# The squares of the norms: all additions but the last of each sum moved from VectorE to GpSimd

## The chip, the core and the metric

The kernel runs on one core of a Trainium2 chip. The time is that of one launch in device microseconds; the number compared is the median of several runs. The core's engines work side by side, each from a queue of its own in a fixed order: TensorE (PE; its weight loads are shown as PEld), VectorE (DVE), ScalarE (ACT), GpSimd (POOL) and SyncE (SP). They wait for each other by semaphores.

## What is computed

The program is three transformer blocks one after the other, over 512 tokens of width 1024 in fp32: a first block with three mixers and a gated feed-forward part, a second with two layers of mixers (sparse attention, convolution, latent attention, delta rule) and feed-forward parts, and a third with two recurrent mixers and a feed-forward part. What matters here is that norms over the 1024 channels stand ahead of and behind nearly every matrix product. Cut to that:

```python
def rmsnorm(x, g):
    xf = x.astype(jnp.float32)
    y = xf * lax.rsqrt(jnp.mean(xf * xf, axis=-1, keepdims=True) + NORM_EPS)
    return (y * g.astype(jnp.float32)).astype(x.dtype)

def layernorm(x, g, b):
    xf = x.astype(jnp.float32)
    mu = jnp.mean(xf, axis=-1, keepdims=True)
    var = jnp.mean(jnp.square(xf - mu), axis=-1, keepdims=True)
    y = (xf - mu) * lax.rsqrt(var + EPS) * g.astype(jnp.float32) + b.astype(jnp.float32)
    return y.astype(x.dtype)

# first block
x = x + rmsnorm(mix, post_mix_g[l])
h = rmsnorm(x, pre_ffn_g[l])
gate, up = jnp.split(h @ w_ffn_in[l], 2, axis=-1)
f = (jax.nn.silu(gate) * up) @ w_ffn_out[l]
x = x + rmsnorm(f, post_ffn_g[l])
# third block
x = _layernorm(ALPHA * x + mixed @ w_out[layer], ln1_g[layer], ln1_b[layer])
```

## The kernel before

Activations are kept transposed: a vector of 512 tokens by 1024 channels is eight tiles of 128 channels by 512 tokens. Around the norms the work is cut into two halves of 256 tokens (`HF`), so that most tiles there are 128x256. Every matrix product is split in three to keep fp32's precision: weights and activations are split into a high part and the rest (`whi`, `wlo`, `ahi`, `alo`), and TensorE multiplies low by high, high by low and high by high (lines 458 to 460, 610 to 612 and 652 to 654). A weight of 128x1024 comes by DMA into `wst`, ScalarE makes `whi` from it (line 525) and VectorE `wlo` (line 534, the helper through which VectorE's two-operand instructions go).

A norm needs the sum over channels, that is over the eight tiles and the 128 partitions of each. The class `Sums` (lines 289 to 394) does it for one half. For each tile `put` makes the square (`sq`, on ScalarE; every second one on VectorE in the first mixer) and holds it back until the next tile's turn, when `up` adds it into an accumulator `nm_as` (128x256). For a layernorm `put` also subtracts a rough mean (`nm_mb`) and a second accumulator `nm_ax` sums the values themselves. `flush` adds the last square held back; then `columns` multiplies the accumulator with a column of ones on TensorE (line 367), and some fifteen small VectorE instructions (`nm_c`, `nm2y`, `nm2t`, `nm2h`) make the reciprocal root. `rows` transposes it back into rows (line 710) for scaling (`nm_r` of an output norm, `fd_rb` of an input norm). The very last norm of the program, in its second half, feeds its last square to TensorE without the last addition (`direct`).

There are 24 such sums, six of them of layernorms (two in the convolution, two each for the two layernorms of block 3). They stand in `boundary` (lines 727 to 830), which ends one stage and begins the next: the output product's halves, their sums, the scaling and adding to `x` (through `po_t` in the first block), the split of the new `x` into `ahi` and `alo` for the next product with its own sum (`Feed`, lines 396 to 438), and the next product's first matmuls (`First`, lines 441 to 465). `boundary` writes these pieces in an order that follows estimated due times; after that the framework schedules instructions by priority and by its own estimate of each one's duration, so a changed instruction can move others in every engine's queue. The first sum of all, at the program's start, is that of the input (`x_in`).

GpSimd does little: some memsets, the DMA issues of six of the convolution's eight tiles (`ud` and `c_x`, lines 1665 and 1668), and six multiplications and additions in the last norm (lines 1798 and 1799). Its first arithmetic instruction is that of the last norm.

Of the kernel before, what the change touches and what calls it, by code (L numbers as in the profile page):

```python
# [15 lines left out]
ALU = mybir.AluOpType  # L16
# [61 lines left out]
def _consts():  # L78
    c = {}
    i = np.arange(P)  # L80
    f = np.float32
    c["ident"] = np.eye(P, dtype=f)
    caus = np.zeros((P, S), f)
    caus[:, S - P:] = np.where(i[None, :] > i[:, None], NEG, 0.0)
    c["caus"] = caus
    j = np.arange(64)
    h = i % 64
    c["eye2"] = (h[:, None] == j[None, :]).astype(f)
    up = [(h[:, None] < j[None, :]), (h[:, None] <= j[None, :])]
    c["upm"] = np.concatenate(up, 1).astype(f)  # L90
    for m in (1, 2, 4, 8, 16, 32):
        t, s = h[:, None], j[None, :]
        same = (t // (2 * m)) == (s // (2 * m))
        c[f"lev{m}"] = (same & ((t // m) % 2 == 1) & ((s // m) % 2 == 0)).astype(f)
    t, s = j[None, :], h[:, None]
    c["lev1T"] = (((t // 2) == (s // 2)) & (t % 2 == 1) & (s % 2 == 0)).astype(f)
    c["eye32"] = (i[:, None] % 32 == np.arange(32)[None, :]).astype(f)
    c["headones"] = ((i[:, None] // 64) == (i[None, :] // 64)).astype(f)
    c["headind"] = ((i[:, None] // 64) == np.arange(2)[None, :]).astype(f)
    c["triu"] = (i[:, None] <= i[None, :]).astype(f)  # L100
    c["reset"] = np.repeat((np.arange(S) % 64 > 0).astype(f)[None], P, 0)
    return c
# [186 lines left out]
class Sums:  # L289
# [22 lines left out]
    def put(self, x):  # L312
        k, i = self.k, self.count
        if self.ln:
            k.tt(x, x, self.mb, ALU.subtract)
        late, self.late = self.late, []
        if not i:
            self.acc["s"] = k.square(self.tile("s"), i, x)
            self.first = x
        else:  # L320
            pool, tags, bufs, _ = self.sqs
            sq = pool.tile([P, self.n], F32, name="sq", tag=tags[i % len(tags)], bufs=bufs)
            self.late.append(("s", k.square(sq, i, x)))
            if self.ln:
                self.late.append(("x", x))
        self.up(late)
        self.count += 1

    def up(self, late):
        k = self.k  # L330
        for what, x in late:
            if what not in self.acc:
                self.acc[what] = self.tile(what)
                k.tt(self.acc[what], self.first, x, ALU.add)
            else:
                k.tt(self.acc[what], self.acc[what], x, ALU.add)

    def flush(self, last=False):

        k, n = self.k, self.n  # L340
        if self.early:
            ps = k.bank(self.psp, "st")
            k.T.matmul(ps[:, :n], k.onesq, self.early[0], start=True, stop=True)
            self.mb = self.sp.tile([P, n], F32, name="nm_mb", bufs=2)
            k.copy(self.mb, ps[:, :n], 1.0 / P)
            for x in self.early:
                self.put(x)
            self.early = []
            yield FL, False
        if last and not self.direct:  # L350
            late, self.late = self.late, []
            self.up(late)

    def rstd(self, eps, out):

# [1945 lines left out]
```

## Time and profile before

| | us |
|---|---|
| median of three runs | 3287.34 |
| lowest and highest | 3286.98, 3298.29 |
| the profiled execution's time | 3295.74 |
| its span in the profile | 3293.7 |
| granted TensorE clock, mean | 0.992 of full speed |
| HBM read and written | 297.45 MB, 7.46 MB |

The page's first lines give each engine's busy time and share of the span. Its chain follows back from the last instruction what each one waited for. A view of waits names who waited for what in how many places; a group view adds up instructions of one line and shape, with busy time and the mean duration of one; a timeline gives start, duration, engine, line and operands, and in brackets the idle time ahead and what ended it. In windows the columns are the busy time of PE, PEld, DVE, ACT and POOL, then the granted TensorE clock.

### The profile page before, as it was taken

The page shows a single profiled execution, that of the slowest core. Times are in us where ns is not written, and L with a number is a line of the kernel's source. Part 1 is how long each engine was busy: PE and PEld are TensorE (multiplying, and loading weights), DVE is VectorE, ACT ScalarE, POOL GpSimd, SP SyncE. Part 2 cuts the span into 40 slices and gives each one's busy share as a digit, 9 for nine tenths or more (in the row PEclk, how much of TensorE's full clock was granted, in tenths as well). Part 3 has the DMA queues.
Part 4 walks back from the last instruction along what each step waited for, and adds up shares of the span by engine and source line. Part 5 has one row for each costly group of instructions (what it writes and reads, how often), then busy time and mean ns, then how long its engine had stood idle before and what let it go on. Part 6 is the DMA issues. An engine that isn't in the chain of part 4 may idle for free.

```text
span 3293.7 us, 47967 instructions
## 1 busy us (share of the span) xinstructions
PE 3238.2 (98%) x19850; PEld 2698.0 (82%) x19850; DVE 1929.5 (59%) x4109; ACT 1177.1 (36%) x1879; POOL 29.3 (1%) x99
## 2 busy tenths in 40 slices
PE   8999999999999999999999999999999999999998
PEld 6877888897879888977888897778787777998888
DVE  7567743458856444597544466574466566563336
ACT  4243533234354222335322243343343433353223
POOL 0000000000000000020000000000000000000000
PEclk9999999999999999999999999999999999999999
DMA  3210522232212222262322231112221222222322
GB/s 137 78 43 5 171 99 102 91 107 79 88 64 77 102 91 102 106 184 93 112 90 102 104 139 62 65 65 90 84 87 62 102 77 103 103 100 90 106 90 90
DMA packets 57354, 308.00 MB, mean 94 GB/s; under 512 B 7088, under 2 KB 16432, under 8 KB 24496
## 3 DMA queue, kind: packets, MB, share of 16 engines
q1 hardware_dynamic: 54736, 296.79, 25.7%
q0 software_dynamic: 2400, 8.16, 1.0%
q8 instruction: 155, 2.54, 0.3%
q14 instruction: 63, 0.52, 0.0%
HBM read 297.45 MB, written 7.46 MB: 93 GB/s over the span
## 4 chain that ended last, share of the span: by engine, by line
PE 94%; DVE 4%; ACT 1%; issue 0%; DMA 0%; POOL 0%; SPq 0%; ACTq 0%; DVEq 0%
PE mm L652 15%; PE mm L653 15%; PE mm L654 15%; PE mm L610 8%; PE mm L612 8%; PE mm L611 8%; PE mm L635 2%; PE mm L637 2%; PE mm L636 2%; PE iv L1203 2%; PE mm L458 1%; PE mm L459 1%; PE mm L460 1%; PE cv L1691 1%; PE sc L2185 1%; PE sc L1975 1%
## 5 line engine op out<-in xcount | busy, mean ns | idle before, releaser
L534 DVE TENSOR_TENSOR wlo<-wst,whi 128x1024 fp32r<-128x1024 f32 (+2 forms) x535 | 646.9, 1212 | 669.5 <-ACT whi L525 668.1
L525 ACT ACTIVATE whi<-wst 128x1024 fp32r<-128x1024 f32 (+2 forms) x535 | 559.6, 1049 | 1217.7 <-PE mm L654 632.0
L652 PE MATMUL mm<-ahi,wlo 128*128 128x512 f32 (+1 forms) x1984 | 726.4, 367 | 2.7 <-DVE x L544 1.9
L653 PE MATMUL mm<-alo,whi 128*128 128x512 f32 (+1 forms) x1984 | 726.8, 367 | 0.2 <-DVE alo L534 0.2
L654 PE MATMUL mm<-ahi,whi 128*128 128x512 f32 (+1 forms) x1984 | 725.2, 366 | 0.0
L652 PEld LDWEIGHTS mm<-ahi,wlo 128*128 128x128 f32 x1984 | 375.1, 189 | 64.3 <-DVE x L544 2.1
L653 PEld LDWEIGHTS mm<-alo,whi 128*128 128x128 f32 x1984 | 375.6, 189 | 62.9 <-issue 2.5
L654 PEld LDWEIGHTS mm<-ahi,whi 128*128 128x128 f32 x1984 | 375.4, 189 | 61.2 <-issue 1.7
L610 PE MATMUL mm<-ahi,wlo 128*128 128x512 f32 (+2 forms) x1048 | 423.3, 404 | 0.5 <-DVE d_qi L534 0.5
L612 PE MATMUL mm<-ahi,whi 128*128 128x512 f32 (+2 forms) x1048 | 408.4, 390 | 0.0
L611 PE MATMUL mm<-alo,whi 128*128 128x512 f32 (+2 forms) x1048 | 406.7, 388 | 0.0
L610 PEld LDWEIGHTS mm<-ahi,wlo 128*128 128x128 f32 (+1 forms) x1048 | 197.1, 188 | 50.0 <-issue 9.3
L612 PEld LDWEIGHTS mm<-ahi,whi 128*128 128x128 f32 (+1 forms) x1048 | 196.9, 188 | 42.1 <-issue 0.2
L611 PEld LDWEIGHTS mm<-alo,whi 128*128 128x128 f32 (+1 forms) x1048 | 197.2, 188 | 39.6 <-issue 2.5
L652 PE MATMUL mm<-hhi,wlo 128*128 128x256 f32 (+1 forms) x720 | 228.4, 317 | 0.0
L653 PE MATMUL mm<-hlo,whi 128*128 128x256 f32 (+1 forms) x720 | 228.1, 317 | 0.0
L654 PE MATMUL mm<-hhi,whi 128*128 128x256 f32 (+1 forms) x720 | 227.1, 316 | 0.0
L458 PE MATMUL mm<-ahi,wlo 128*128 128x256 f32 x512 | 144.0, 290 | 16.7 <-DVE wlo L534 10.3
L459 PE MATMUL mm<-alo,whi 128*128 128x256 f32 x512 | 146.4, 288 | 1.6 <-DVE alo L544 1.5
L460 PE MATMUL mm<-ahi,whi 128*128 128x256 f32 x512 | 145.2, 286 | 0.0
L653 PEld LDWEIGHTS mm<-hlo,whi 128*128 128x128 f32 x720 | 137.4, 191 | 8.9
L652 PEld LDWEIGHTS mm<-hhi,wlo 128*128 128x128 f32 x720 | 137.2, 191 | 9.2
(471 smaller groups left out, 4418.3 us busy)
## 6 DMA issues: line engine op xcount, KB each, us to landing
wst<-in_w2f SPq DMA_DIRECT2D x36, 1024.0 KB, 4.8
wst<-in_w2i SPq DMA_DIRECT2D x32, 1024.0 KB, 4.8
wst<-in_w1i SPq DMA_DIRECT2D x22, 1024.0 KB, 4.9
wst<-in_w3f SPq DMA_DIRECT2D x22, 1024.0 KB, 4.9
wst<-in_w1f SPq DMA_DIRECT2D x10, 1024.0 KB, 4.8
wst<-in_w3d SPq DMA_DIRECT2D x10, 1024.0 KB, 4.9
wst<-in_w1o SPq DMA_DIRECT2D x8, 1024.0 KB, 4.9
wst<-in_w2qk SPq DMA_DIRECT2D x8, 1024.0 KB, 4.9
```

Source lines behind the costliest of these rows:

```text
L458: K_.T.matmul(ps, lo[:, c], ah, start=k == 0, stop=False)
L459: K_.T.matmul(ps, hi[:, c], al, start=False, stop=False)
L460: K_.T.matmul(ps, hi[:, c], ah, start=False, stop=k == KD - 1)
L525: return self.A.activation(out, in_, func, **kw)
L534: return self.V.tensor_tensor(out, a, b, op=op)
L610: self.T.matmul(ps, lo[:, c], ah, start=k == 0, stop=False)
L611: self.T.matmul(ps, hi[:, c], al, start=False, stop=False)
L612: self.T.matmul(ps, hi[:, c], ah, start=False, stop=k == n - 1)
L635: self.T.matmul(ps, ah[:, c], lo, start=k == 0, stop=False)
L652: self.T.matmul(ps, lo[:, c], ah, start=k == 0, stop=False)
L653: self.T.matmul(ps, hi[:, c], al, start=False, stop=False)
L654: self.T.matmul(ps, hi[:, c], ah, start=False, stop=k == n - 1)
```

## The change

`up` gets the engine that adds as an argument. `put` passes GpSimd (`k.G`), `flush` passes VectorE (`k.V`) for the last addition of each sum. The instruction is written out instead of going through the helper at line 534; what that helper adds, a raised priority, was not in force at these places.

```diff
@@ put
-        self.up(late)
+        self.up(late, k.G)
         self.count += 1
 
-    def up(self, late):
-        k = self.k
+    def up(self, late, e):
         for what, x in late:
             if what not in self.acc:
                 self.acc[what] = self.tile(what)
-                k.tt(self.acc[what], self.first, x, ALU.add)
+                e.tensor_tensor(self.acc[what], self.first, x, op=ALU.add)
             else:
-                k.tt(self.acc[what], self.acc[what], x, ALU.add)
+                e.tensor_tensor(self.acc[what], self.acc[what], x, op=ALU.add)
@@ flush
         if last and not self.direct:
             late, self.late = self.late, []
-            self.up(late)
+            self.up(late, k.V)
```

In instructions: of 208 additions on VectorE 180 go to GpSimd (144 into `nm_as`, 36 into `nm_ax`), 28 stay. VectorE's queue falls from 4063 to 3883 instructions, GpSimd's grows from 104 to 284. GpSimd's set-up instruction for arithmetic moves from ahead of the last norm to the start of its queue. Lines behind 329 are one lower after the change.

The first place is the first boundary, where the output product of the first block's mixers meets the feed-forward part. VectorE before (`nm_as_4374` sums the second half of the output, `nm_as_4371` the first half of the new `x`):

```order
L544 SCALAR_TENSOR_TENSOR po_t_4532<-y6_4241,vec1_80,nm_r0_4359 128x256
L534 TENSOR_TENSOR nm_as_4371<-nm_as_4371,sq_4517 128x256
L534 TENSOR_TENSOR x6_4212<-x6_4212,po_t_4532 128x256
L544 SCALAR_TENSOR_TENSOR po_t_4554<-y7_4242,vec1_80,nm_r0_4359 128x256
L534 TENSOR_TENSOR nm_as_4374<-nm_as_4374,sq_4483 128x256
L544 SCALAR_TENSOR_TENSOR alo_4536<-x6_4212,vec1_80,ahi_4535 128x256
L534 TENSOR_TENSOR x7_4213<-x7_4213,po_t_4554 128x256
L534 TENSOR_TENSOR nm_as_4371<-nm_as_4371,sq_4539 128x256
L534 TENSOR_TENSOR nm_as_4374<-nm_as_4374,sq_4577 128x256
L544 SCALAR_TENSOR_TENSOR alo_4558<-x7_4213,vec1_80,ahi_4557 128x256
L534 TENSOR_TENSOR nm_as_4371<-nm_as_4371,sq_4561 128x256
L534 TENSOR_TENSOR nm_as_4374<-nm_as_4374,sq_4581 128x256
```

VectorE at the same place after the change:

```order
L543 SCALAR_TENSOR_TENSOR po_t_4532<-y6_4241,vec1_80,nm_r0_4359 128x256
L543 SCALAR_TENSOR_TENSOR po_t_4554<-y7_4242,vec1_80,nm_r0_4359 128x256
L543 SCALAR_TENSOR_TENSOR alo_4514<-x5_4211,vec1_80,ahi_4513 128x256
L533 TENSOR_TENSOR x6_4212<-x6_4212,po_t_4532 128x256
L533 TENSOR_TENSOR x7_4213<-x7_4213,po_t_4554 128x256
L543 SCALAR_TENSOR_TENSOR alo_4536<-x6_4212,vec1_80,ahi_4535 128x256
L543 SCALAR_TENSOR_TENSOR alo_4558<-x7_4213,vec1_80,ahi_4557 128x256
L335 TENSOR_TENSOR nm_as_4371<-nm_as_4371,sq_4561 128x256
```

Only the last addition of the feed's sum is left among these rows; the others, of both sums, stand in GpSimd's queue in turns, one chain between the other. On TensorE the matmuls with ones of these sums (line 367) move forward, from behind 2606 and 2618 instructions to behind 2583 and 2596. At the program's start that of the first sum moves from behind 52 to behind 33.

The second place is the end of the first layernorm's sums in block 3. VectorE before (`nm_as_25318` and `nm_ax_25359` are the two accumulators of its second half):

```order
L534 TENSOR_TENSOR nm_as_25318<-nm_as_25318,sq_25463 128x256
L534 TENSOR_TENSOR nm_ax_25359<-nm_ax_25359,x3_24870 128x256
L544 SCALAR_TENSOR_TENSOR x1_24868<-x1_24868,mm_25478 128x256
L534 TENSOR_TENSOR alo_25489<-x7_24874,ahi_25488 128x256
L534 TENSOR_TENSOR x1_24868<-x1_24868,nm_mb_25315 128x256
L534 TENSOR_TENSOR nm_as_25318<-nm_as_25318,sq_25536 128x256
L534 TENSOR_TENSOR nm_ax_25359<-nm_ax_25359,x0_24867 128x256
L534 TENSOR_TENSOR nm_as_25318<-nm_as_25318,sq_25542 128x256
L534 TENSOR_TENSOR nm_ax_25359<-nm_ax_25359,x1_24868 128x256
```

VectorE there after the change:

```order
L533 TENSOR_TENSOR wlo_25563<-wst_25556,whi_25562 128x1024
L533 TENSOR_TENSOR alo_25489<-x7_24874,ahi_25488 128x256
L533 TENSOR_TENSOR x0_24867<-x0_24867,nm_mb_25315 128x256
L543 SCALAR_TENSOR_TENSOR x1_24868<-x1_24868,mm_25478 128x256
L533 TENSOR_TENSOR x1_24868<-x1_24868,nm_mb_25315 128x256
L335 TENSOR_TENSOR nm_ax_25359<-nm_ax_25359,x1_24868 128x256
L335 TENSOR_TENSOR nm_as_25318<-nm_as_25318,sq_25542 128x256
```

One addition of each accumulator is left, and a weight split (`wlo`) has come in ahead of them.

The third place is GpSimd's queue in the convolution, where its DMA issues stand (`ud` is a copy of a gated tile `c_u` in HBM, `c_x` the reordered tile that TensorE's taps read; `y` are the taps' results). After the change:

```order
L1664 DMA ud_13276<-c_u_13273 128x542
L335 TENSOR_TENSOR nm_as_13256<-nm_as_13256,sq_13259 128x256
L333 TENSOR_TENSOR nm_ax_13385<-y0_12989,y1_12990 128x256
L335 TENSOR_TENSOR nm_as_13266<-nm_as_13266,sq_13269 128x256
L333 TENSOR_TENSOR nm_ax_13391<-y0_12989,y1_12990 128x256
L1664 DMA ud_13398<-c_u_13395 128x542
L335 TENSOR_TENSOR nm_as_13256<-nm_as_13256,sq_13382 128x256
L1667 DMA c_x_13275<-ud_13276 32x4x528 x4
L1667 DMA c_x_13397<-ud_13398 32x4x528 x4
```

Before the change only two memsets (`c_u`) stand between these DMA issues; five additions have come in ahead of the first issue of `c_x_13275`.

## The prediction

> **What bounds the kernel now.** I read the page's engine totals and its chain first, then the waits of TensorE (PE), then short windows.
>
> ```profile
> PE 3238.2 (98%) x19850; PEld 2698.0 (82%) x19850; DVE 1929.5 (59%) x4109; ACT 1177.1 (36%) x1879; POOL 29.3 (1%) x99
> PE 94%; DVE 4%; ACT 1%; issue 0%; DMA 0%; POOL 0%; SPq 0%; ACTq 0%; DVEq 0%
> ```
>
> TensorE is busy for 3238.2 of the span's 3293.7 us. Only 55.5 us of the span are idle on it, and no relief of another engine can win more than that. VectorE (DVE) is 59% busy and GpSimd (POOL) 1%, so most of what VectorE does ends behind matmuls. The next view tells which part of the 55.5 us hangs on VectorE (total, times, longest).
>
> ```profile
> PE mm L458 <- DVE wlo L534: 10.3, 2, 9.2
> PE mm L458 <- ACT ahi L525: 5.0, 4, 2.3
> PE st L367 <- DVE nm_as L534: 4.0, 4, 1.9
> PE st L710 <- DVE nm_o L544: 3.7, 2, 2.4
> ```
>
> The 9.2 us of the first row lie ahead of the first matmul, where weights are still loading. The others lie at ends of norms. Two places hold most of what an add can reach. Each row of the next view gives width, busy time of PE, PEld, DVE, ACT, POOL, then clock, DMA share and GB/s.
>
> ```profile
> 0.00:40.00 40.00, 28.87 (x211) 27.54 (x212) 29.80 (x88) 21.57 (x39) 0.50 (x7) 1.00 0.62 228
> 343.00:400.00 57.00, 50.77 (x399) 48.19 (x398) 46.66 (x141) 32.62 (x70) 0.00 (x0) 0.94 0.49 172
> 735.00:800.00 65.00, 62.55 (x421) 54.21 (x419) 56.63 (x169) 31.96 (x64) 0.00 (x0) 1.00 0.32 109
> 2880.00:2930.00 50.00, 47.88 (x393) 46.95 (x392) 43.45 (x132) 26.70 (x55) 0.00 (x0) 1.00 0.24 86
> 376.00:382.00 6.00, 6.00 (x52) 6.00 (x51) 6.00 (x18) 3.75 (x10) 0.00 (x0) 1.00 0.56 195
> ```
>
> At the first boundary (343 to 400) TensorE idles 57 − 50.77 = 6.2 us, and in the last row VectorE is busy without a gap just ahead of that. At the first layernorm of block 3 (2880 to 2930) TensorE idles 2.1 us with VectorE 87% busy, at the boundary 735 to 800 2.5 us with 87%.
>
> **What is removed, and what it costs now.** The groups of the adds (count | busy, mean ns):
>
> ```profile
> L534 DVE TENSOR_TENSOR nm_as<-nm_as,sq 128x256 f32<-128x256 f32 x167 | 70.0, 423 | 2.7
> L534 DVE TENSOR_TENSOR nm_ax<-nm_ax,x 128x256 f32<-128x256 f32 x23 | 9.7, 422 | 0.0
> L534 DVE TENSOR_TENSOR nm_ax<-nm_ax,y 128x256 f32<-128x256 f32 x12 | 5.1, 423 | 0.1
> L534 DVE TENSOR_TENSOR nm_ax<-x,x 128x256 f32<-128x256 f32 x4 | 1.7, 424 | 0.0
> L1798 POOL TENSOR_TENSOR x<-x,nm_r 128x256 f32<-128x256 f32 x3 | 2.1, 727 | 561.1 <-ACT nm_r L525 561.1
> ```
>
> The program has 208 such adds, 206 of them in these rows; 28 stay on VectorE and 180 move. A recorded 423 ns overlaps the next instruction; the step from one start to the next is what a queue pays:
>
> ```profile
> 377.91 0.76 DVE L534 TENSOR_TENSOR nm_as<-nm_as,sq 128x256 f32<-128x256 f32 x2
> 378.58 0.48 DVE L544 SCALAR_TENSOR_TENSOR alo<-x,vec,ahi 128x256 fp32r<-128x256 f32 x1
> 3284.40 1.41 POOL L1798 TENSOR_TENSOR x<-x,nm_r 128x256 f32<-128x256 f32 x2 [561.08 <-ACT nm_r L525]
> 3285.76 1.41 POOL L1799 TENSOR_TENSOR x<-x,nm_r 128x256 f32<-128x256 f32 x2
> 3284.34 0.75 DVE L1798 TENSOR_TENSOR x<-x,st 128x256 f32<-128x256 f32 x2 [0.94 <-ACT nm_r L525]
> 3285.01 0.75 DVE L1799 TENSOR_TENSOR x<-x,st 128x256 f32<-128x256 f32 x2
> ```
>
> Two VectorE adds take 378.58 − 377.91 = 0.67, so 0.335 us each: 180 × 0.335 = 60 us leave VectorE. Two GpSimd instructions of the same shape take 3285.76 − 3284.40 = 1.36, so 0.68 each: 180 × 0.68 = 122 us come to GpSimd. That engine is busy for 29.3 us in all, so it has the room. A chain of six adds (4.1 us) is slower there than on VectorE (2.0 us) only if the squares come faster than one in 0.68 us.
>
> **What of it lies on the path.** At the first boundary:
>
> ```profile
> 384.29 0.43 DVE L534 TENSOR_TENSOR nm_as<-nm_as,sq 128x256 f32<-128x256 f32 x1
> 386.54 0.45 PE L710 MATMUL st<-ct,fd_c 128*128 128x128 f32 x2 [0.52 <-DVE fd_c L544]
> 388.32 0.66 PE L710 MATMUL st<-ct,nm_o 128*128 128x128 f32 x2 [1.33 <-DVE nm_o L544]
> 391.25 1.22 PE L458 MATMUL mm<-ahi,wlo 128*128 128x256 f32 x4 [2.27 <-ACT ahi L525]
> ```
>
> The last add of the output's sum, at 384.29, opens a chain (root, transposes, scaling, `ahi`) at whose end TensorE waits 0.5 + 1.3 + 2.3 = 4.1 us. Ahead of that add VectorE runs without a gap, with 11 moved adds (3.7 us) in it. The layernorm in block 3 is alike:
>
> ```profile
> 2917.03 0.42 DVE L534 TENSOR_TENSOR nm_as<-nm_as,sq 128x256 f32<-128x256 f32 x1
> 2917.37 0.42 DVE L534 TENSOR_TENSOR nm_ax<-nm_ax,x 128x256 f32<-128x256 f32 x1
> 2918.90 0.16 DVE L539 TENSOR_SCALAR nm_c<-st 128x4 f32<-128x4 f32 x1 [1.11 <-PE st L367]
> PE mm L458 <- ACT ahi L525: 2.0, 1, 2.0
> ```
>
> There 2.0 us of waiting for `ahi` follow. At the start and in the convolution:
>
> ```profile
> 14.58 0.28 PE L460 MATMUL mm<-ahi,whi 128*128 128x256 f32 x1
> 14.70 0.28 PE L458 MATMUL mm<-ahi,wlo 128*128 128x256 f32 x1
> 16.59 0.43 DVE L534 TENSOR_TENSOR nm_as<-nm_as,sq 128x256 f32<-128x256 f32 x1
> 26.14 0.38 PE L458 MATMUL mm<-ahi,wlo 128*128 128x256 f32 x1 [1.07 <-DVE wlo L534]
> PE mm L459 <- DVE alo L544: 1.5, 3, 0.7
> 1520.41 0.35 PE L367 MATMUL st<-ones,nm_as 128*128 128x1 f32 x2 [1.72 <-DVE nm_as L534]
> ```
>
> The start holds 1.07 of waiting for `wlo` and two of the three waits for `alo`, 1.5 − 0.7 = 0.8; the convolution's last norm 1.7. All together an add can reach 4.1 + 2.0 + 1.9 + 1.7 = 9.7 us. Everywhere else the matmuls run on over the norms, and the 60 us win nothing.
>
> **Moved and added waits.** The order of TensorE's queue shifts: the norm matmuls of line 367 stand 19 matmuls earlier in the first sum and 22 or 23 earlier at the first boundary. At the start TensorE then stands at the norm's matmul near 14.6 us (the row at 14.58), while VectorE ends its last add of that sum, less five before it, near 16.59 + 0.335 − 5 × 0.335 = 15.25; the 0.65 us lost there are won back from the later waits of the start. Behind that matmul in TensorE's queue stand only matmuls of the same projection. At the first boundary 23 matmuls by 0.12 (14.70 − 14.58) are 2.8 us, and VectorE's 11 adds less are 3.7: TensorE comes no earlier than the sum. Each sum now ends with VectorE waiting for GpSimd; queued behind that last add stand splits (`alo`, `wlo`). No row shows that handover; the nearest is VectorE's wait for TensorE's small sum:
>
> ```profile
> 383.69 0.16 DVE L540 TENSOR_SCALAR nm_c<-st 128x2 f32<-128x2 f32 x1 [0.36 <-PE st L367]
> ```
>
> Its ends are 0 and one GpSimd step, 0.68. I take 0.2 us, under the 0.36 of this row since the matmul's own time is in it. At some eight sums that TensorE waits for, this makes 8 × 0.2 = 1.6 us (0 to 5.4).
>
> GpSimd's queue also issues the convolution's DMAs:
>
> ```profile
> 1468.80 2.18 POOL L1668 DMA_DIRECT2D c_x<-ud  x4 [2.87 <-DMA ud<-c_u]
> 1481.08 1.50 PE L1691 MATMUL cv<-c_x,c_dg 128*32 128x512 f32 x12
> ```
>
> At most five adds (3.4 us) stand ahead of these issues now. Issued at 1468.8 and landing in about 6.4 us, they have 1481.1 − 1468.8 − 6.4 = 5.9 us to spare, so nothing shows. In the final norm two early adds move, while TensorE still has output matmuls: nothing either way.
>
> **The unknown cost.** No row shows a VectorE instruction with two operands in SBUF beside a GpSimd instruction. The VectorE rows at 3284.34, with one operand in PSUM, keep 0.335 us beside GpSimd: one end is 0 per add. The other end is that VectorE stands still for GpSimd's whole step, 0.68. Between them: if both engines read through something that carries VectorE's two operands in 0.335 us, an add takes that much of it whoever asks. The two ends are equally far from that, the row nearest in kind lies at 0 but has only one operand in SBUF, so I take the middle, 0.34: VectorE loses what it saved, 180 × (0.34 − 0.335), about nothing. The sum is then 0 + 1.6 us on the profiled execution (3295.7 us; 3293.7 of span and 2.0 around it). The median shown is 3287.3, 8.4 below the profiled one; the same 1.6 us on it make 3288.9, **3289**. With a cost of 0.17 instead of 0.34 per add it is half of the first rival's gain (−4), with 0.51 half of the second one's loss (+8): own range 3283 to 3297.
>
> **Rivals.**
> - *Side by side* (cost 0 per add). VectorE is then ahead at the boundaries: 3.7 of the 4.1 us at the first, 2.0 at the layernorm, 0.8 at the start, 1.5 in the convolution: 8.0 us, so 3279. For it speaks the unslowed VectorE row beside GpSimd; against it, that row's PSUM operand.
> - *Turn by turn* (cost 0.68 per add, and the slower side). Each moved add delays VectorE by 0.68 − 0.335 = 0.345 us net. It decides where VectorE is over some 75% busy at a boundary and TensorE has no slack: at the start (29.80 of 40), at 343, 735 and 2880. With 12 adds in each, 4 × 12 × 0.345 = 16.6 us, so 3304. For it speaks that nearly all of VectorE's work around the adds has two SBUF operands; against it, that GpSimd may as often be the one that waits. The Trainium skill, in "SBUF — State Buffer", section "Who interferes with whom", says that a VectorE instruction with two SBUF inputs and a GpSimd instruction that reads SBUF shut each other out for the whole instruction, whichever comes first. It speaks against this change, and no row here shows it; by it the time is this rival's, by the unslowed row at 3284.34 the first one's.
> - *A late first add.* GpSimd's first arithmetic comes at about 8 us instead of 3284. If it needs preparation that isn't over by then, the first norm is late by as much and TensorE waits us for us; at 4 us late, 3289 + 4 = 3293. Against it: the engine's set-up instruction stands at its queue's start, some 7 us ahead. The Trainium skill, "GPSIMD Engine Reference", section "2.1 Instruction dispatch", gives about 6 us for a first call; by it this would just be covered, and no run here shows it.
>
> **How the numbers follow.** Forecast 0.45, side by side 0.27, turn by turn 0.24, late first add 0.04. The range of 8 in 10 reaches to 3277 (side by side, with 2 us for the execution's own spread) and to 3308 (turn by turn with some handovers). 0.5% is 16.4 us, about what a measurement can tell from no change: under 3270.9 lies only a side-by-side case that wins elsewhere too (0.03); over 3303.8 half of turn by turn and a little of the rest (0.15); between them 0.82.
>
> **What would show it.** GpSimd's adds at 0.68 us steps and VectorE's two-operand instructions stretched by about half a GpSimd step: the forecast. VectorE's steps at 0.335 beside GpSimd, and the wait for `ahi` near 391 gone: side by side. VectorE instructions of 0.7 to 1.1 us beside the adds, and new TensorE waits for `nm_as` or `alo` at 343, 735 and 2880: turn by turn. GpSimd's first add later than 9 us: the late start. The prediction is wrong as a whole if GpSimd's step is far from 0.68, or if a late sum holds TensorE at line 367 for several us at many norms.

## The result, and the profile after

The changed kernel takes 3326.85 us (median; 3323.77 to 3330.29) against 3287.24 us before, a ratio of 1.011 with an interval of [1.0097, 1.0123]: some 36 us slower by the ratio (32 to 40 by its interval). The forecast was 3289, its range ended at 3308. The profiled execution after took 3323.77 us with a span of 3322.0, 28.3 more than the span of before.

The page of the changed kernel, its engine totals:

```profile
PE 3242.4 (98%) x19850; PEld 2703.1 (81%) x19850; DVE 1923.0 (58%) x3929; ACT 1177.7 (35%) x1879; POOL 197.9 (6%) x279
```

TensorE's idle time grew from 55.5 to 3322.0 − 3242.4 = 79.6 us. VectorE lost 180 instructions, 60 us of steps, and is busy for only 6.5 us less than before: the 1929.5 became 1923.0. GpSimd is busy for 169 us more, where 180 instructions of the last norm's 727 ns would make 131. TensorE's waits in the changed kernel (total, times, longest):

```profile
PE st L366 <- DVE nm_as L335: 12.7, 13, 2.6
PE mm L457 <- DVE wlo L533: 9.2, 1, 9.2
PE cv L1690 <- DMA c_x<-ud: 6.4, 1, 6.4
PE mm L651 <- DVE x L543: 5.5, 1, 5.5
PE mm L457 <- DVE y L533: 4.1, 2, 2.6
PE mm L457 <- DVE x L543: 3.8, 3, 1.7
PE mm L458 <- DVE alo L543: 3.8, 4, 1.8
```

The wait for a sum (line 366 now) went from 4.0 us in 4 places to 12.7 in 13, and waits for `c_x`, `x` and `y` are new or longer. The groups of the same trace show both engines stretched:

```profile
L335 POOL TENSOR_TENSOR nm_as<-nm_as,sq 128x256 f32<-128x256 f32 x144 | 135.6, 944 | 1640.1 <-ACT sq L524 1606.2 <-ACT nm_as L524 25.5 <-DVE nm2t L543 2.5
L335 POOL TENSOR_TENSOR nm_ax<-nm_ax,x 128x256 f32<-128x256 f32 x20 | 20.9, 1045 | 16.9 <-DVE x L533 16.4
L543 DVE SCALAR_TENSOR_TENSOR alo<-x,vec,ahi 128x256 fp32r<-128x256 f32 x80 | 55.1, 711 | 3.7 <-ACT ahi L524 3.7
L533 DVE TENSOR_TENSOR ff_u<-mm,fd_rb 128x512 f32<-128x512 f32 x86 | 58.7, 690 | 66.2 <-PE mm L653 62.4 <-PE mm L459 3.8
```

GpSimd's addition takes 944 to 1045 ns instead of the 727 of the last norm. VectorE's `alo`, which stands between the additions at every boundary and reads two tiles of SBUF, went from 482 ns to 711. `ff_u<-mm,fd_rb`, with an operand in PSUM, has 690 ns as before. The two groups in the trace of before:

```profile
L544 DVE SCALAR_TENSOR_TENSOR alo<-x,vec,ahi 128x256 fp32r<-128x256 f32 x80 | 36.8, 482 | 1.2 <-ACT ahi L525 1.2
L534 DVE TENSOR_TENSOR ff_u<-mm,fd_rb 128x512 f32<-128x512 f32 x86 | 58.7, 690 | 66.2 <-PE mm L654 62.4 <-PE mm L460 3.8
```

A piece of the convolution's timeline shows it at its most extreme (start, duration, engine, line, operands; the last row is of a view by tile):

```profile
1456.75 0.75 POOL L335 TENSOR_TENSOR nm_as<-nm_as,sq 128x256 f32<-128x256 f32 x1
1457.44 0.75 POOL L333 TENSOR_TENSOR nm_ax<-y,y 128x256 f32<-128x256 f32 x1
1458.14 0.74 POOL L335 TENSOR_TENSOR nm_as<-nm_as,sq 128x256 f32<-128x256 f32 x1
1458.84 0.73 POOL L333 TENSOR_TENSOR nm_ax<-y,y 128x256 f32<-128x256 f32 x1
1455.53 6.58 DVE L543 SCALAR_TENSOR_TENSOR y<-c_u,vec,y 128x512 f32<-128x512 f32 x5
L543 DVE SCALAR_TENSOR_TENSOR y<-c_u,vec,y x68: 474/746/3810, 1414.8 to 1507.2; 128x512 f32<-128x512 f32 x60, 128x256 f32<-128x256 f32 x8
```

The five VectorE instructions need 5.88 / 8 = 0.73 us each, less in a stream, some 3.4 in all (eight of them take 5.88 in the trace of before); beside four GpSimd additions they took 6.58. The last row gives the shortest, middle and longest of this group: one instruction lasted 3.81 us, about 3.1 more than usual. Four additions, 2.8 us, went by while a single VectorE instruction stood. Here the price of an addition to VectorE is 0.7 to 0.8 us, not 0.34.

That place is an exception. Of the 110 VectorE instructions that the changed kernel's trace shows stretched by more than 0.15 us, this one alone spans four additions; the others span one or two. Summed up by place (each duration less the usual one of its group in the trace of before), VectorE loses 0.45 us for each addition at the program's start, 0.35 at the first boundary, 0.42 at the next one, 0.30 in the convolution and 0.29 at the first layernorm of block 3.

To see where the 28 us lie, the table gives TensorE's lag: the start of a matmul in a run's profiled execution less the start of the same matmul (counted in order, without the norms' small ones) in that of before. The heads of the columns are times of the trace of before. A positive number is later; the last column is what is added after the last matmul. The runs below are in it too.

| run | 316 us | 459 | 729 | 837 | 1468 | 1567 | 2874 | 2989 | tail |
|---|---|---|---|---|---|---|---|---|---|
| the change | −1.3 | 4.4 | 4.4 | 7.9 | 9.1 | 19.3 | 20.2 | 23.7 | 4.1 |
| additions left out | −4.9 | −11.9 | −11.9 | −15.7 | −16.4 | −9.1 | −9.7 | −12.1 | 0.0 |
| unread additions beside | 3.0 | 12.6 | 12.6 | 19.7 | 21.2 | 30.8 | 31.2 | 37.9 | 4.8 |
| the same, memsets moved | 3.7 | 13.3 | 13.3 | 20.3 | 21.9 | 24.7 | 25.1 | 31.7 | 4.8 |
| free memsets, memsets moved | −6.0 | −5.9 | −5.9 | −5.8 | −5.6 | −5.6 | −5.4 | −5.4 | −0.8 |
| layernorm sums back | 2.4 | 10.5 | 10.5 | 14.9 | 15.9 | 16.0 | 16.8 | 16.8 | 0.0 |
| layernorm sums only | −5.1 | −5.1 | −5.1 | −5.0 | −4.5 | 5.5 | 5.5 | 9.0 | 3.5 |

The change loses at the first boundary (316 to 459: 5.7 us), at the next one (3.5), across the convolution (10.2), at the first layernorm of block 3 (3.5) and in the last norm (4.1). Between these places the lag hardly moves. The program's start has a loss too, which the first column hides: a column at 40 us would show the changed kernel 3.8 us late, but from 40 to 100 us the trace of before has a granted clock of 0.91, where the changed kernel has the full clock, and falls back by 5 us. (The profiled execution of before is itself 8.4 us over the median, which is why even runs that equal it in the median stand at −5 here.)

### The profile page after: what moved, and what is told of

Read it like the earlier page. It is cut to its first block, busy times and chain, and to the rows that moved or that the text cites. A ratio compares the mean times of both kernels' runs of the same rounds, so it can differ in the third digit from the quotient of the medians.

```text
span 3322.0 us, 48091 instructions
## 1 busy us (share of the span) xinstructions
PE 3242.4 (98%) x19850; PEld 2703.1 (81%) x19850; DVE 1923.0 (58%) x3929; ACT 1177.7 (35%) x1879; POOL 197.9 (6%) x279
## 4 chain that ended last, share of the span: by engine, by line
PE 51%; DVE 3%; ACT 0%; issue 0%; POOL 0%; DMA 0%; SPq 0%; ACTq 0%; POOLq 0%; DVEq 0%
PE mm L651 7%; PE mm L652 7%; PE mm L653 7%; PE mm L609 6%; PE mm L611 6%; PE mm L610 6%; PE mm L634 1%; PE mm L636 1%; PE mm L635 1%; PE sc L2184 1%; PE sc L1974 1%; DVE wlo L533 1%; PE pw L2033 1%; PE mm L457 1%; PE mm L458 1%; PE mm L459 1%
## 5 line engine op out<-in xcount | busy, mean ns | idle before, releaser
L335 POOL TENSOR_TENSOR nm_as<-nm_as,sq 128x256 f32<-128x256 f32 x144 | 135.6, 944 | 1640.1 <-ACT sq L524 1606.2
```

The lines of the kernel that those rows point to most:

```text
L335: e.tensor_tensor(self.acc[what], self.acc[what], x, op=ALU.add)
```

## The experiments

These are the theories that the experiments set against each other. Theory A is turn by turn: a GpSimd addition and a VectorE instruction with two inputs in SBUF exclude each other. Theory B: the changed order of the queues costs the time. Theory C: GpSimd's chain of additions is too slow, or its handover to VectorE. Theory D came later, with the run that led to it. All ratios are to the kernel before, run beside.

**Additions left out.**

```diff
-        self.up(late, k.G)
+        self.up([(what, t) for what, t in late if what not in self.acc], k.V)
```

> The additions that the change moved are left out (six that open an accumulator of a layernorm stay on VectorE), so the norms' sums hold only the first and the last square of each; GpSimd does none. TensorE's queue stands as after the change (norm matmuls after 33, 87, 2425, 2583 ... instructions). Theory A, turn by turn (a GpSimd addition and a VectorE instruction with two inputs in SBUF exclude each other): without GpSimd's additions nothing is lost, and VectorE is relieved, 3277 to 3287 us. Theory B, the changed order of the queues costs the time: 3310 to 3330 us. Theory C, GpSimd's chain of additions is too slow or the handover to VectorE is: the chain is gone, 3277 to 3287, as by A.

Measured: 3281.04 us, ratio 0.997 [0.9961, 0.9979]; in the profile 12.1 us less than before. VectorE's group of `alo` is back at its length:

```profile
PE 3231.2 (98%) x19850; PEld 2695.6 (82%) x19850; DVE 1873.2 (57%) x3935; ACT 1176.1 (36%) x1879; POOL 29.3 (1%) x99
L543 DVE SCALAR_TENSOR_TENSOR alo<-x,vec,ahi 128x256 fp32r<-128x256 f32 x80 | 36.5, 482 | 3.6 <-ACT ahi L524 3.5
PE mm L651 <- DVE x L543: 6.8, 1, 6.8
```

VectorE's 1873.2 is 49.8 us less than in the changed kernel, which has six additions fewer on VectorE: so GpSimd's 180 additions stretch VectorE's work by about 52 us, 0.29 each on the mean of all places. Theory B falls as the whole cause, for the order is that of the change but for a few per cent of the instructions, and the kernel is faster. But it holds in one place: across the convolution this run loses 7.3 us without any GpSimd addition (−16.4 to −9.1). TensorE waits there 6.8 us for `x`: the rows of VectorE that take results out of PSUM (`x<-mm,vec,x`) now stand behind the scalings of the second half. In the timeline of this run, and then of before:

```profile
1520.13 2.77 DVE L533 TENSOR_TENSOR y<-y,nm_r 128x256 f32<-128x256 f32 x8
1523.48 0.88 DVE L543 SCALAR_TENSOR_TENSOR x<-mm,vec,x 128x256 f32<-128x256 f32 x2
```

```profile
1527.63 0.48 DVE L544 SCALAR_TENSOR_TENSOR x<-mm,vec,x 128x256 f32<-128x256 f32 x1
1529.76 1.09 DVE L534 TENSOR_TENSOR y<-y,nm_r 128x256 f32<-128x256 f32 x3
```

The changed kernel has the same wait, 5.5 us.

**Unread additions beside.** The kernel before, and after each addition on VectorE one on GpSimd that nobody needs (two for layernorms):

```diff
                 k.tt(self.acc[what], self.acc[what], x, ALU.add)
+            if beside and what == "s":
+                for _ in range(1 + self.ln):
+                    k.G.tensor_tensor(x, x, x, op=ALU.add)
```

> The kernel before, all additions on VectorE, and beside them 180 additions on GpSimd that nothing reads (each adds a square's tile to itself when VectorE has used it). TensorE's queue stands as before the change. Theory A: VectorE keeps its own additions and stands still for GpSimd's as well, 0.68 us each instead of 0.345 net: at least the loss of the change, 3325 to 3365 us. Theory B (order): 3285 to 3295. Theory C (late sums, handover): no sum waits for GpSimd, 3285 to 3295.

Measured: 3339.0 us, ratio 1.015 [1.0134, 1.0165], more than the change itself loses. No sum waits for GpSimd, and TensorE's order is that of before but for about a hundred of its 19850 matmuls; C falls as the main cause, and A stands.

**Free memsets beside.** As above, but `k.G.memset(x, 0.0)` twice in place of each addition.

> As the run with additions beside, but GpSimd only writes: two memsets of 128x256 (about 0.3 us each) in place of each addition, 360 in all. If what excludes is reading of SBUF by both engines: 3285 to 3295 us, and VectorE's instructions keep their length. If any work of GpSimd beside VectorE costs it: 3310 to 3365.

Measured: 3298.39 us, ratio 1.0028 [1.0016, 1.0039]. That is at neither value. VectorE's instructions kept their length, so it isn't contention; TensorE's waits show a single new one of that size:

```profile
PE cv L1694 <- DMA c_x<-ud: 9.0, 1, 9.0
```

That led to theory D, tested below: the convolution's own memsets, which clear the padding of `c_u` and stand in GpSimd's queue, wait behind the new work.

**The contention by itself.** A kernel of eight stretches, chains of instructions on tiles of 128x256:

```python
add = lambda d, w: V.tensor_tensor(d, d, src[:, :n], op=ADD)
addp = lambda d, w: V.tensor_tensor(d, d, pb, op=ADD)        # pb in PSUM
gadd = lambda p: G.tensor_tensor(p, p, src[:, :n], op=ADD)
phase("alone", add, gadd, 24, 0)
phase("both", add, gadd, 24, 12)
phase("psum", addp, gadd, 24, 12)
```

> The transformer is left out; eight stretches one after the other measure steps from start to start on tiles of 128x256: 24 VectorE additions alone; 12 GpSimd additions alone; 24 and 12 side by side, with VectorE's second input in SBUF, in PSUM, with one input only (multiply by a constant), with the three-operand form; 24 VectorE additions beside 24 GpSimd memsets; 8 VectorE subtractions of 128x1024 beside 12 GpSimd additions. Theory A: VectorE 0.335 alone, GpSimd 0.68 alone; side by side with two inputs in SBUF 24 x 0.335 + 12 x 0.68 = 16.2 us until both are done; with PSUM, one input or memset no loss, 8.2 us. Sharing element by element (the forecast of the prediction): 12 to 13 us. Side by side: 8.2 us everywhere.

Measured in one execution, in the order alone (VectorE), alone (GpSimd), both, PSUM, memset, 128x1024 beside additions:

```profile
4.57 11.41 DVE L2296 TENSOR_TENSOR d_alone<-d_alone,src 128x256 f32<-128x256 f32 x24
18.01 9.52 POOL L2301 TENSOR_TENSOR p_galone<-p_galone,src 128x256 f32<-128x256 f32 x12
28.93 16.24 DVE L2296 TENSOR_TENSOR d_both<-d_both,src 128x256 f32<-128x256 f32 x24
29.55 10.28 POOL L2301 TENSOR_TENSOR p_both<-p_both,src 128x256 f32<-128x256 f32 x12
46.64 10.90 DVE L2297 TENSOR_TENSOR d_psum<-d_psum,pb 128x256 f32<-128x256 f32 x24
47.20 9.55 POOL L2301 TENSOR_TENSOR p_psum<-p_psum,src 128x256 f32<-128x256 f32 x12
92.55 11.40 DVE L2296 TENSOR_TENSOR d_memset<-d_memset,src 128x256 f32<-128x256 f32 x24
106.27 13.16 DVE L2300 TENSOR_TENSOR w_split<-big,src 128x1024 fp32r<-128x1024 f32 x8 [0.94 <-ACT big L2281]
105.99 16.48 POOL L2301 TENSOR_TENSOR p_split<-p_split,src 128x256 f32<-128x256 f32 x12
```

With PSUM or beside memsets VectorE loses nothing (10.90 and 11.40 against 11.41), and GpSimd nothing beside PSUM operands (9.55 against 9.52). With two inputs in SBUF, VectorE's 24 additions take 16.24: 4.83 us more for 12 GpSimd additions, 0.40 each. The 16.2 us expected by A came out, but not by its sum: a chain's steps are 0.46 and not 0.335 here, since each addition waits for the one before, so the alone times were mis-stated, and some of the exclusion hides in the gaps. In the single instructions of the trace the two engines take turns one for one: while GpSimd works both step by 0.86 us, and VectorE by 0.46 afterwards.

Beside long VectorE instructions both lose: GpSimd needs 16.48 us instead of 9.52, an addition lasting up to 1.59 instead of 0.72, and VectorE's subtraction lasts 1615 ns in the mean, against 1225 for the same form (`wlo`) in the trace of before. The stretch with one input (13.90 us) has its comparison in itself, since GpSimd is done before VectorE. The group of its instructions beside GpSimd (59.7 to 69.2 us), then without (69.26 to 72.9):

```profile
L2298 DVE TENSOR_SCALAR d_one<-d_one 128x256 f32<-128x256 f32 x12 | 9.2, 766 | 0.4
L2298 DVE TENSOR_SCALAR d_one<-d_one 128x256 f32<-128x256 f32 x11 | 3.2, 294 | 0.4
```

So a multiplication by a constant, with a single input in SBUF, pays as well: 766 ns instead of 294, which theory A did not expect. The three-operand form goes from 0.83 to 0.48 us in the same way.

**Parts of the change.** With an attribute for the engine in `Sums`:

```diff
+        self.e = k.G                   # "convolution back": VectorE for its two sums
+        self.e = k.V if ln else k.G    # "layernorm sums back"
+        self.e = k.G if ln else k.V    # "layernorm sums only"
-        self.up(late, k.G)
+        self.up(late, self.e)
```

> The changed kernel, but the convolution's two sums (24 additions) are back on VectorE; 156 stay on GpSimd. In the changed kernel's trace TensorE falls behind the trace of before by 10 us across the convolution (9 us behind at its start, 19 us at its end). Theory A (the loss lies where GpSimd's additions stand beside VectorE): these 10 us come back, about 3317 us. Theory B (order): the run with additions left out lost 7 us there too; if that order stays, only 3 us come back, about 3323.

> The changed kernel, but all six layernorm sums (72 additions) are back on VectorE; 108 stay on GpSimd. By places in the trace: convolution 10, first layernorm of block 3 3.5, end of the last norm 4 us come back: about 3309 us. If the losses do not add up by place, something common to all (the start of the queue, the clock) costs it, and it stays above 3318.

> The kernel before with only the six layernorm sums' 72 additions on GpSimd; all sums of squares alone are on VectorE. The other half of the pair: if losses add up by place, before plus 10 + 3.5 + 4, about 3307 us, and this run's loss plus that of the run with the layernorm sums back is the whole loss of the change.

Measured: convolution back 3313.51 us (1.0073 [1.0056, 1.0089]); layernorm sums back 3309.64 (1.0062 [1.0047, 1.0077]); layernorm sums only 3309.06 (1.0063 [1.0048, 1.0078]). The losses add up by place: 0.62% + 0.63% is 1.25%, with some 0.15 either way on each, and the change has 1.1% [0.97, 1.23]. With the convolution back, more than the 10 us came back, and with it went the wait of 5.5 us for `x`: VectorE's order there is that of before again. In the run with the layernorm sums back the tail's loss is 0.0: the last norm's 4.1 us came with GpSimd's additions.

**DMAs from SyncE.** `q = G if m < 6 else self.nc.sync` becomes `q = self.nc.sync`, in the changed kernel.

> The changed kernel, but all of the convolution's DMAs are issued by SyncE's queue instead of GpSimd's (six tiles' ud and c_x move). TensorE waited 6.4 us once for c_x. If that wait came from the additions ahead of the issues in GpSimd's queue: 3320 us. If it came from VectorE, which made c_u late beside GpSimd's additions: no gain, 3324 to 3330, and the wait stays or moves to another name.

Measured: 3337.34 us, ratio 1.0141 [1.0125, 1.0157], some 10 us worse than the change; TensorE now waits 10.2 us for `ud` there. The other queue is the worse one; since it brings a wait of its own, this run does not tell what the additions ahead of GpSimd's issues cost. The changed kernel's trace does for its wait of 6.4 us. GpSimd's last issue, the issues of SyncE's queue (SPq) in question, and TensorE's wait:

```profile
1479.93 2.18 POOL L1667 DMA_DIRECT2D c_x<-ud  x4 [0.68 <-DMA ud<-c_u]
1504.00 2.13 SPq L1667 DMA_DIRECT2D c_x<-ud  x4
1511.56 1.07 PE L1690 MATMUL cv<-c_x,c_dg 128*32 128x256 f32 x7 [6.42 <-DMA c_x<-ud]
```

All of GpSimd's transfers have landed by 1490 us; what TensorE waits for until 1511.56 is one of the two tiles that SyncE's queue issues anyway. GpSimd's additions did not stand ahead of these issues.

**The padding memsets.** `G.memset(u[:, :W - 1], 0.0)` in the convolution becomes `self.V.memset(...)`: in the changed kernel, in both runs with idle work beside, and in the kernel before as a control.

> The changed kernel, but the memset of each convolution tile's 30 padding columns (c_u, eight in all) is on VectorE instead of GpSimd. In the changed kernel the last two of them end at 1486 and 1491 us, behind additions in GpSimd's queue, 13 and 18 us later against the matmuls than before, and TensorE waits 6.4 us for c_x of these tiles. Theory D (the memsets stuck behind additions make the convolution late): the 6.4 us go and the loss across the convolution falls from 10 to about 4, so 3320 us. Theory A alone (contention makes VectorE late): no gain, 3325 to 3330.

> The run with 360 idle GpSimd memsets beside, with the convolution's eight padding memsets on VectorE as well. That run lost 8 us, 9.0 of waiting for c_x with it. Theory D: the loss was the padding memsets' place in the queue; now 3286 to 3293, like the kernel before, and writing on GpSimd costs VectorE nothing. Otherwise 3297 to 3300 again.

> The run with 180 unread additions on GpSimd beside, with the convolution's eight padding memsets on VectorE as well, so that its queues stand like those of the run with free memsets. What it loses against that run is what reading by GpSimd beside VectorE costs and nothing else. Theory A: 3325 to 3335, at least 35 us. If the queue's order was the larger part: under 3310.

> The kernel before with only the eight padding memsets moved to VectorE: the control for the three runs above. 3286 to 3293.

Measured:

| run | us | ratio, interval |
|---|---|---|
| the change, memsets moved | 3326.75 | 1.0103 [1.0086, 1.0121] |
| free memsets beside, memsets moved | 3289.64 | 0.9991 [0.998, 1.0001] |
| unread additions beside, memsets moved | 3333.27 | 1.0124 [1.0108, 1.0141] |
| before, memsets moved | 3292.14 | 0.9995 [0.9985, 1.0005] |

Theory D is right for the run with free memsets: its loss is gone. For the change it is not what sets the time. The wait for `c_x` shrank from 6.4 to 3.4 us, but the waits behind it took its place. In the convolution's second part (1480 to 1570 us) the changed kernel waited 6.4 us for `c_x`, 5.5 for `x` and 2.3 for sums; with the memsets moved it is:

```profile
PE mm L651 <- DVE x L543: 6.8, 1, 6.8
PE st L366 <- DVE nm_as L335: 4.1, 2, 2.0
PE cv L1690 <- DMA c_x<-ud: 3.4, 1, 3.4
```

The second and third run are the cleanest pair: the same queues, and GpSimd at work beside. Where it only writes, the kernel is as fast as before; where it reads, 3333.27 − 3289.64 = 43.6 us slower, 0.24 us for each of 180 additions. The engine totals of the two, free memsets and then additions:

```profile
PE 3231.5 (98%) x19850; PEld 2693.1 (82%) x19850; DVE 1929.3 (59%) x4117; ACT 1177.2 (36%) x1879; POOL 136.6 (4%) x451
PE 3255.0 (98%) x19850; PEld 2710.2 (81%) x19850; DVE 1977.2 (59%) x4117; ACT 1177.3 (35%) x1879; POOL 174.0 (5%) x271
```

VectorE's own work is stretched by 47.9 us. Of the 43.1 us between the spans (3287.5 and 3330.6), TensorE is idle for 19.6 more; the other 23.5 are its own instructions, longer at a mean granted clock of 0.988 instead of 0.995. Against the kernel before with memsets moved (0.993) it is 19.5 and 17.6. So about half of the price is paid as a slower clock. Most of the loss in clock stands at the start, the boundaries and the last norm, where TensorE waits too; what makes the clock dip, no run here tests.

VectorE's groups of the two, free memsets and then additions:

```profile
L547 DVE SCALAR_TENSOR_TENSOR alo<-x,vec,ahi 128x256 fp32r<-128x256 f32 x80 | 36.6, 478 | 1.2 <-ACT ahi L528 1.2
L537 DVE TENSOR_TENSOR nm_as<-nm_as,sq 128x256 f32<-128x256 f32 x167 | 69.3, 419 | 2.9
```

```profile
L547 DVE SCALAR_TENSOR_TENSOR alo<-x,vec,ahi 128x256 fp32r<-128x256 f32 x80 | 42.1, 546 | 1.2 <-ACT ahi L528 1.2
L537 DVE TENSOR_TENSOR nm_as<-nm_as,sq 128x256 f32<-128x256 f32 x167 | 84.8, 511 | 2.9
```

No run beats both kernels with the sums intact: what the kernel gains from 174 additions less on VectorE is 10 us, and GpSimd's price for them is over 40.

By place, in the table of lags, gain, price and order add up to the change's loss nearly everywhere. At the second boundary the additions of the cleanest pair cost 6.9 us and the additions left out gain 3.8, which makes 3.1 (the change: 3.5); at the first layernorm of block 3 it is 6.6 − 2.4 = 4.2 (3.5). In the convolution the pair costs only 2.8; the larger part of the change's 10.2 are the 7.3 that the new order alone loses. At the first boundary 9.5 − 7.0 = 2.5 falls short of the 5.7. There VectorE is no busier than before (97.3 us against 96.9), and TensorE's new waits are for two sums, 4.5 us together: the late chain of theory C has a share at this place.

## Why the prediction was wrong, point by point

- **What bounds the kernel** was right: TensorE, and of other engines only what ends last at a boundary. Every us lost is idle time of TensorE at the norms, or a slower clock beside it, for which the prediction had no term. Against the trace of before TensorE's busy time grew by 4.2 us; in the window from 0 to 40 the granted clock was 0.96 instead of 1.00. In the cleanest pair the clock is about half of the loss.
- **The relief** (reach 9.7 us, of which 8.0) was about right: with the additions left out the median fell by some 10 us. It lay elsewhere in part: 7.0 us at the first boundary instead of 3.7, of which 3.5 are TensorE's idle time (7.6 to 4.1) and the rest its own time at the full clock instead of 0.96; 3.8 at the next one, which had no term; and 7.3 us of it were lost again in the convolution.
- **The unknown cost** is the step that failed: "VectorE loses what it saved, 180 × (0.34 − 0.335), about nothing". As a size for VectorE, 0.34 was near: 0.29 on the mean of all places, 0.29 to 0.45 at the five places told above, 0.40 in the chains, and VectorE's busy time did stay level (1929.5 to 1923.0). What failed is reading a level VectorE as a level kernel. Some 60 us taken off VectorE gain the kernel 10, with the new order's loss in the convolution already in it; the 48 us by which GpSimd's reading stretches VectorE cost it 43.6. The reason for the middle, a path shared element by element, is refuted too, so that the near size is luck: beside 128x1024 subtractions a 128x256 addition of GpSimd lasts up to 1.59 us instead of 0.72, so it waits out the long instruction, and with a single input in SBUF VectorE pays as well.
- **The reach of a loss.** The sum netted the cost against the saving over all 180 additions, and then had only the handovers left. The table of lags shows why the two sides did not cancel. A loss isn't bounded by the idle time that a gain could reach: the start, the boundary at 735 to 800 and the tail turned from covered to late. (In the convolution it was the order more than the cost.)
- **GpSimd's step**, 0.68, is 0.70 where the convolution's two chains alternate, but 0.80 in a single chain of the small kernel, alone and beside PSUM operands; and beside VectorE its additions last 0.94 to 1.05 in the mean. The handover, put at 1.6 us (0 to 5.4), shows 3.4 us of VectorE's idle time ahead of the last additions:

```profile
L335 DVE TENSOR_TENSOR nm_as<-nm_as,sq 128x256 f32<-128x256 f32 x23 | 9.5, 416 | 4.2 <-POOL nm_as L335 3.4 <-POOL l_u L2114 0.6
```

  The chain is late too: TensorE waits for sums at 13 places, not 8, and "TensorE comes no earlier than the sum" fails with it: at the first boundary it waits 4.5 us for two of them.
- **The convolution's DMAs** ("nothing shows"): for GpSimd's issues that held, as the changed kernel's trace shows: the tile waited for is one of SyncE's. But two things there were missed. VectorE's reordered queue puts the evictions of `x` behind the second half's scalings; that alone lost 7.3 us with the additions left out. And GpSimd's padding memsets ended at 1486 and 1491 behind additions; they delayed `c_x`, yet with them moved the time stayed, since the waits for `x` and for the sums grew.
- **The tail** ("nothing either way") lost 4.1 us. The chain's end in the changed kernel's timeline:

```profile
3303.52 0.74 DVE L533 TENSOR_TENSOR x<-x,nm_mb 128x256 f32<-128x256 f32 x1
3302.46 1.53 POOL L335 TENSOR_TENSOR nm_as<-nm_as,sq 128x256 f32<-128x256 f32 x2
3303.94 0.90 POOL L335 TENSOR_TENSOR nm_ax<-nm_ax,x 128x256 f32<-128x256 f32 x1
3304.81 0.72 POOL L335 TENSOR_TENSOR nm_as<-nm_as,sq 128x256 f32<-128x256 f32 x1
3309.19 0.16 DVE L538 TENSOR_SCALAR nm_c<-st 128x4 f32<-128x4 f32 x1 [4.93 <-PE st L366]
```

  VectorE is through with the last tile at 3304.3; GpSimd still adds until 3305.5, and the sum reaches VectorE at 3309.2, after sixteen small matmuls that follow each other in 0.21 us here and in 0.11 before. All additions of this `direct` sum but the left-out last run on GpSimd, in its time.
- **The rival turn by turn** had the right mechanism, with a chance of 0.24, but not the right sum. Its price of 0.68 an addition was too high, 0.29 to 0.45 being measured; its 3304 was too low all the same, since it counted four places with 12 additions at 0.345 net. It lacked the convolution, the tail and the clock, and netted the saving against the cost. The rule of the Trainium skill in "SBUF — State Buffer", section "Who interferes with whom", held in the three forms that have a comparison: two SBUF inputs against a reading GpSimd instruction (loss), one PSUM operand (none), a GpSimd memset that only writes (none). The multiplication by a constant, which lost, is not of the form that the prediction took from it.
- **The late first add** did not come: GpSimd's first addition starts at 6.73 us and takes 0.72.

Open is what decides the turns: in the chains and beside long subtractions the engines alternate one for one (GpSimd lost 8% and 73%, VectorE 42% in the chains), yet in the convolution VectorE once stood for four additions on end. Open is also why the clock dips, and how much of the first boundary's loss is the late chain.

## What to carry to other kernels

An idle engine isn't free if it reads through what a busy one needs: before moving VectorE work to GpSimd, look at what VectorE does beside it. Two-input instructions on SBUF tiles pay for it, and so did a multiplication of one SBUF tile by a constant; an operand in PSUM and write-only GpSimd work didn't. Don't net such a cost against a saving on the same engine: what is taken off an engine that is mostly covered wins little, and what is added to it can make covered places late. Look at the order too: in the convolution it cost more than the contention. And an experiment with the moved work left out, and one with it doubled beside and unread, take apart what the move gains (10 us here) and what it costs (43.6, against the same run with memsets in place of the additions).

## What was not expected of the hardware

One VectorE instruction of 0.75 us lasted 3.81 while four GpSimd additions went by: the wait isn't always limited to one instruction of the other engine. In the other direction, 12 GpSimd additions took 16.48 instead of 9.52 us beside 128x1024 subtractions on VectorE. A VectorE multiplication with a single SBUF input lasted 766 ns beside GpSimd's additions and 294 without. And between two kernels with the same VectorE order, TensorE's own busy time grew by 23.5 us at a lower granted clock, more than its idle time (19.6).
